# Earlier sums of x, block products for every gate pair, and low weight parts added by DMA in a two-layer hybrid decoder

## The chip, the cores and the metric

The kernel runs on one core of one Trainium2 chip. The metric is device time in microseconds (us) of one execution, the median of several runs; smaller is better. Besides the time there is a profile of one execution, with a trace of every instruction.

## The reference

Two layers work on x of 512 tokens by 1024 channels, in float32. Each layer makes one wide projection of x and feeds three mixers with it:

```python
z = einsum('bsd,de->bse', x, w_in[l])          # 1024 -> 6816 columns
(q_lat, kv_lat, k_pe, g_mla, lru_u, g_lru, r_q, r_k, r_v, g_ret, merge_logits) = split(z)
y_mla = mla(q_lat, kv_lat, k_pe, ...) * silu(g_mla)       # latent attention, 8 heads
y_lru = rglru(lru_u, ...) * silu(g_lru)                   # convolution and linear recurrence
y_ret = retention(r_q, r_k, r_v, ...) * silu(g_ret)       # 8 heads, chunks of 128 tokens
gates = sigmoid(merge_logits + b_merge[l])                # 3 x 1024 columns
mixed = sum over n of gates[n] * (y_n @ w_branch[l, n])   # each 512 -> 1024
x = layer_norm(ALPHA * x + mixed @ w_out[l])
```

## The kernel before, in words

**Three products for one.** A float32 operand is held as a high part (rounded to fp32r by a copy) and a low part (the operand less its high part). `mm3` makes high x high, high x low and low x high, so each product of tiles is three matmuls. `split` makes the two parts: a copy on ACT (L113) and a subtraction on DVE (L114). Weights come from HBM in chunks of 128 x 1024 (`load_w`): a DMA on SP's queue into a raw tile `wr` (three buffers), then `split` into `wh` and `wl` (four buffers each).

**A plain projection** of 128 output columns (`in_tile`) loads one chunk and runs 8 x 3 matmuls of 512 columns into one PSUM bank, `psmm`.

**A projection by seven products** (`in_pair`, fed by `Blocks`) makes two such tiles together in Strassen's manner. x, stored transposed as `xth`/`xtl`, is cut into four blocks: channel half k by token half t. Seven products of 12 matmuls of 256 columns each (84) replace 8 x 3 x 2 = 48 matmuls of 512. They go in the order a11, a12, s1, s2, s3, s4, a22, with two branch products b1 and b0 between them. Products a11, a12 and a22 use blocks of x as they are; s1 to s4 use four sums of such blocks, the tiles `tx`, in the order 0 to 3. `x_sums` makes these once in a layer, in four steps: each some additions on DVE (L330, L333) over 128 x 1024 elements, then `split`. The weights of s1 to s4 are sums too: two SP DMAs and one POOL DMA that adds to what is there (L383) make them in `ws`, DVE adds once more (L410), and each half chunk is split. Three PSUM tiles, `psx`, `psy1` and `psz`, are open during a pair.

**Stages of a layer.** Latent projections (`psg`); the four convolution tiles T_U; transposes of the latents (`psl`, read by DVE into `qll`/`ll`, L553); the gates T_GM and T_GL; the recurrence on ACT and DVE; queries and keys (`psq`, `psk`); attention, with the retention's values `psv` among it; retention; the gates and branches; the output projection with layer norm. In the retention's loop (`for q in range(6)`) `ret_in` makes keys and queries of two heads (tiles T_RK + t, T_RQ + t) and their rotation on DVE, `ret_keys` the scores (`psrs`, masked into `sd`), `ret_states` the running states on DVE (L757, L759), `ret_out` the output `por`.

After this loop the first four of the eight lru output tiles are made with plain projections (`in_tile` and `branch_mm`), and one step of `x_sums` stands after each; then twelve pairs by seven products follow.

**Memory.** PSUM has three pools: `ps_mm` (three banks, for `psmm`, `psx`, `psy1`, `psz`, `por`), `ps_s` (three, for `psq`, `psk`, `psb`, scores) and `ps_t` (two, for transposes). The choice between the first two is made in `PS` by the name. SBUF tiles come from rings by size: `wide` (five), `half` (four), `slot` (thirteen). A tile can be taken when an older one of its ring has had its last reader. `x_sums` takes two `wide` and four `half` before; in the retention the halves hold `rts[0..3]`, and the wides `ym`, `vr`, `tabs`, `yr`.

**Order.** A scheduler lays down each engine's instruction list when the kernel is built. It goes by the order of the code, takes what its cost model holds to be ready, and under `high_priority(offset=n)` treats instructions as if they stood n places earlier. On the chip each engine, and each DMA queue's issuer, runs its list in order and waits where an input or a buffer isn't ready.

Of the kernel before, what the change touches and what calls it, by code (L numbers as in the profile page):

```python
# [12 lines left out]
F32R = mybir.dt.float32r  # L13
# [5 lines left out]
P = 128  # L19
# [54 lines left out]
def trunk(ctx, tc, x_in, xt_in, pos, vecs, wg, wt, wrv, wuq, wuk, wuv, wlru, wbr, wout, lng, lnb, dec, rett, out):  # L74
# [37 lines left out]
    def split(hi, lo, src):  # L112
        nc.scalar.copy(hi, src)  # L113
        nc.vector.tensor_tensor(out=lo, in0=src, in1=raw(hi), op=ALU.subtract)  # L114

    def load_w(src, n, dst=None, ahead=True, dma=None, r=None):
        with tc.high_priority(offset=OFF if ahead else 0):
            if r is None:
                r = wraw.tile([P, 1024], F32, tag="wr", name="wr")
                (dma or nc.sync).dma_start(out=r[:, :n], in_=src)  # L120
            if dst is None:
                dst = (whl.tile([P, 1024], F32R, tag="wh", name="wh"), whl.tile([P, 1024], F32R, tag="wl", name="wl"))
            hi, lo = dst
            split(hi[:, :n], lo[:, :n], r[:, :n])
        return hi, lo

    def mm3(ps, lhs, rhs, start, stop, more=False):
# [170 lines left out]
    def layer(l):  # L298
        def in_tile(t):

            hi, lo = load_w(wt[l, t], 1024)
            ps = ps_mm.tile([P, S], F32, tag="mm", name="psmm")
            for k in range(KD):
                c = slice(k * P, (k + 1) * P)
                mm3(ps, (hi[:, c], lo[:, c]), xt[k], k == 0, k == KD - 1)
            return ps
# [8 lines left out]
            return [(xth[:, HK * k + j, HS * t:HS * t + HS], xtl[:, HK * k + j, HS * t:HS * t + HS]) for j in range(HK)]  # L315

        def sums(i):
            return [(tx[i][:, j, :HS], tx[i][:, j, HS:]) for j in range(HK)]

        def x_sums(tiles, scratch):  # L320

            tx[:] = tiles
            (r1, r2), (d, r4) = [(raw(t[:, :, :HS]), raw(t[:, :, HS:])) for t in scratch]

            def b(k, t):
                o = (slice(None), slice(HK * k, HK * k + HK), slice(HS * t, HS * t + HS))
                return raw(xth[o]), raw(xtl[o])

            def sub(out, a, c, op=ALU.subtract):
                nc.vector.tensor_tensor(out=out, in0=a, in1=c, op=op)  # L330

            def neg_less(out, a, c):
                nc.vector.scalar_tensor_tensor(out=out, in0=a, scalar=-1.0, in1=c[0], op0=ALU.mult, op1=ALU.subtract)  # L333
                sub(out, out, c[1])

            def less(out, a, c):
                sub(d, a[1], c[1])
                sub(out, a[0], c[0])
                sub(out, out, d, ALU.add)

            def done(i, r):
                split(tx[i][:, :, :HS], tx[i][:, :, HS:], r)

            def one():
                less(r1, b(0, 0), b(0, 1))
                done(0, r1)

            def two():
                neg_less(r2, r1, b(1, 1))
                done(1, r2)  # L350

            def three():
                less(r1, b(1, 1), b(0, 1))
                done(2, r1)

            def four():
                neg_less(r4, r2, b(1, 0))
                done(3, r4)

            return [one, two, three, four]  # L360

        class Blocks:


            def __init__(self, jobs, two):
                self.pairs = jobs
                self.two = two
                order = ("a11", "a12", "s1", "s2", "b1", "s3", "b0", "a22", "s4")
                self.jobs = [(n, m) for n, (_, wb) in enumerate(jobs) for m in order if wb is not None or m[0] != "b"]
                self.used = self.made = self.loaded = 0  # L370
                self.raws, self.ready, self.free = [], [], []

            def load(self):
                n = self.loaded
                if n == len(self.pairs):
                    return
                self.loaded += 1
                t, wb = self.pairs[n]
                d = {}
                s = self.two[:, n % 2 * 2:n % 2 * 2 + 2, :]  # L380
                nc.sync.dma_start(out=s[:, 0, :], in_=wt[l, t + 1][:, 512:])
                nc.sync.dma_start(out=s[:, 1, :], in_=wt[l, t][:, :512])
                nc.gpsimd.dma_start(out=s, in_=wt[l, t + 1][:, :512].unsqueeze(1).to_broadcast([P, 2, 512]), accum_op=ALU.add)  # L383
                d["s1"] = d["s2"] = d["s4"] = s[:, 0, :]
                d["s3"] = s[:, 1, :]
# [218 lines left out]
        for c in range(3):  # L604
            hi, lo = load_w(wuq[l, c], 768)
            for j in range(2):
                t = 2 * c + j
                ps = PS("psq")
                for k in range(3):
                    w = slice((j * 3 + k) * P, (j * 3 + k + 1) * P)  # L610
                    mm3(ps, (hi[:, w], lo[:, w]), qlat[k], k == 0, k == 2)
# [161 lines left out]
        for q in range(6):  # L773
            if q < 4:
                ret_in(q)
            if 0 <= q - 1 < 4:
                ret_keys(q - 1)
                ret_states(q - 1)
            if 0 <= q - 2 < 4:
                ret_out(q - 2)  # L780


        mixed = [slot("mixed") for _ in range(KD)]
# [23 lines left out]
            nc.gpsimd.tensor_tensor(out=rv, in0=vv, in1=mhalf, op=ALU.pow)  # L807
            nc.vector.tensor_tensor(out=y3, in0=y3, in1=rv.unsqueeze(2).to_broadcast([P, H, 64]), op=ALU.mult)


        scratch = [half("sx", F32R) for _ in range(2)]
        steps = x_sums([wide("tx", F32R) for _ in range(2)] + [half("tx", F32R) for _ in range(2)], scratch)
        for d2 in range(2):
            w = load_w(wbr[l, 1, d2], 1024)
            for j in range(2):
                d = 2 * d2 + j
                psg = in_tile(T_ME + KD + d)
                gt = slot("gt")
                nc.scalar.activation(gt, psg, AF.Sigmoid, bias=v(l, V_BM + KD + d))
                nc.vector.tensor_tensor(out=mixed[d], in0=branch_mm(w, j, yl), in1=gt, op=ALU.mult)  # L820
            steps[2 * d2]()
            steps[2 * d2 + 1]()

        def me(b, d2):
            return T_ME + b * KD + 2 * d2, wbr[l, b, d2]

        def gr(c2):
            return T_GR + 2 * c2, None

        bs = Blocks([me(1, 2), me(1, 3), me(0, 0), me(0, 1), gr(0), me(0, 2), gr(1), me(0, 3)] + [me(2, d2) for d2 in range(4)], wide("ws"))  # L830
        with tc.high_priority(offset=OFF):
            bs.load()
            bs.upto(AHEAD)
# [51 lines left out]

        yhi, ylo = half("ymh", F32R), half("yml", F32R)
        ymp = [(yhi[:, c, :], ylo[:, c, :]) for c in range(4)]
        for i in range(2):
            gate_pair(1, 2 + i, yl)
            norm_rows(i)  # L890
            for c in (2 * i, 2 * i + 1):
                split(ymp[c][0], ymp[c][1], ym[:, c, :])
# [168 lines left out]
```

## Time and profile before

| What | Value |
|---|---|
| median of 3 runs | 1042.44 us (1042.44 to 1042.65) |
| the profiled execution's own time | 1044.03 us |
| its span, first to last instruction | 1042.2 us |
| PE (TensorE matmul) busy | 1028.0 us, 99%, 6135 matmuls |
| DVE (VectorE) busy | 826.6 us, 79% |
| ACT (ScalarE) busy | 507.2 us, 49% |
| POOL (GpSimd) busy | 89.3 us, 9% |
| mean granted TensorE clock | 0.998 of full |

Matmuls are pipelined and the profile models their ends, so one matmul's duration overlaps the next one's; what a matmul costs in a full stream is the distance between starts. A row of the timeline has the start, the length, the engine, the line and what was done; a bracket at its end names how long the engine idled and what released it.

### The profile page before, as it was taken

The page shows a single profiled execution, that of the slowest core. Times are in us where ns is not written, and L with a number is a line of the kernel's source. Part 1 is how long each engine was busy: PE and PEld are TensorE (multiplying, and loading weights), DVE is VectorE, ACT ScalarE, POOL GpSimd, SP SyncE. Part 2 cuts the span into 40 slices and gives each one's busy share as a digit, 9 for nine tenths or more (in the row PEclk, how much of TensorE's full clock was granted, in tenths as well). Part 3 has the DMA queues.
Part 4 walks back from the last instruction along what each step waited for, and adds up shares of the span by engine and source line. Part 5 has one row for each costly group of instructions (what it writes and reads, how often), then busy time and mean ns, then how long its engine had stood idle before and what let it go on. Part 6 is the DMA issues. An engine that isn't in the chain of part 4 may idle for free.

```text
span 1042.2 us, 16322 instructions
## 1 busy us (share of the span) xinstructions
PE 1028.0 (99%) x6135; PEld 901.2 (86%) x6135; DVE 826.6 (79%) x1586; ACT 507.2 (49%) x963; POOL 89.3 (9%) x133
## 2 busy tenths in 40 slices
PE   9999999999999999999999999999999999999997
PEld 8877788888889999998898787888888999999986
DVE  6998989878967787687656889997789667877765
ACT  4549576511535555463223695674115445555510
POOL 1100012000102100001001000120000121000010
PEclk9999999999999999999999999999999999999999
DMA  8232431122455556525233224211214655665321
GB/s 260 81 101 86 132 112 41 43 85 76 118 149 160 160 162 195 143 91 212 75 120 102 76 78 158 79 42 63 80 62 121 206 139 140 166 201 146 120 100 61
DMA packets 46639, 123.55 MB, mean 119 GB/s; under 512 B 5088, under 2 KB 8032, under 8 KB 46560
## 3 DMA queue, kind: packets, MB, share of 16 engines
q1 hardware_dynamic: 38592, 105.39, 30.4%
q0 software_dynamic: 7680, 16.78, 8.3%
q8 instruction: 48, 0.79, 0.3%
q10 hardware_dynamic: 288, 0.34, 0.2%
q14 instruction: 31, 0.25, 0.1%
HBM read 116.20 MB, written 4.19 MB: 116 GB/s over the span
## 4 chain that ended last, share of the span: by engine, by line
PE 79%; DVE 11%; ACT 5%; issue 2%; DMA 2%; POOL 0%; SPq 0%; DVEq 0%; ACTq 0%; POOLq 0%
PE psmm L129 6%; PE psmm L130 5%; PE psmm L131 5%; PE psx L129 5%; PE psx L131 4%; PE psx L130 4%; PE psb L129 4%; PE psb L130 4%; PE psb L131 4%; PE pso L130 3%; PE pso L129 3%; PE pso L131 3%; PE psz L130 2%; PE psz L131 2%; PE psz L129 2%
## 5 line engine op out<-in xcount | busy, mean ns | idle before, releaser
L113 ACT CAST wh<-wr 128x512 fp32r<-128x512 f32 (+4 forms) x202 | 157.4, 789 | 217.4 <-PE psmm L130 122.0
L114 DVE TENSOR_TENSOR wl<-wr,wh 128x512 fp32r<-128x512 f32 (+4 forms) x202 | 179.7, 898 | 38.6 <-ACT wh L113 37.8
L129 PE MATMUL psmm<-xth,wh 128*128 128x512 f32 x384 | 151.3, 394 | 0.1
L130 PE MATMUL psmm<-xtl,wh 128*128 128x512 f32 x384 | 150.3, 391 | 0.0
L131 PE MATMUL psmm<-xth,wl 128*128 128x512 f32 x384 | 150.1, 391 | 0.0
L114 DVE TENSOR_TENSOR wl<-ws,wh 128x512 fp32r<-128x512 f32 x96 | 66.1, 689 | 46.2 <-ACT wh L113 45.4
L113 ACT CAST wh<-ws 128x512 fp32r<-128x512 f32 x96 | 59.5, 620 | 72.9 <-PE psx L130 37.8
L129 PEld LDWEIGHTS psmm<-xth,wh 128*128 128x128 f32 x384 | 72.2, 188 | 14.8 <-issue 0.4
L131 PEld LDWEIGHTS psmm<-xth,wl 128*128 128x128 f32 x384 | 72.1, 188 | 14.8
L130 PEld LDWEIGHTS psmm<-xtl,wh 128*128 128x128 f32 x384 | 72.2, 188 | 14.2
L129 PE MATMUL psx<-tx,wh 128*128 128x256 f32 x288 | 82.3, 286 | 0.3
L131 PE MATMUL psx<-tx,wl 128*128 128x256 f32 x288 | 81.5, 283 | 0.0
L130 PE MATMUL psx<-tx,wh 128*128 128x256 f32 x288 | 81.5, 283 | 0.0
L383 POOL DMA_DIRECT2D ws<-in_wt x24 | 29.1, 1220 | 399.6 <-DMA ws<-in_wt 225.9
L129 PEld LDWEIGHTS psx<-tx,wh 128*128 128x128 f32 x288 | 54.9, 191 | 4.9 <-ACT cg L446 1.1
L130 PEld LDWEIGHTS psx<-tx,wh 128*128 128x128 f32 x288 | 55.0, 191 | 1.6
L131 PEld LDWEIGHTS psx<-tx,wl 128*128 128x128 f32 x288 | 55.0, 191 | 0.0
L663 ACT ACTIVATE pr<-pss,nm 128x128 f32<-128x128 f32 (+1 forms) x64 | 34.0, 531 | 19.3 <-DVE nm L658 18.6
L656 PE MATMUL pss<-kt,qt 96*128 96x128 f32 (+3 forms) x128 | 42.1, 435 | 0.0
L129 PE MATMUL psg<-wh,xth 128*128 128x336 f32 x128 | 41.3, 323 | 0.0
L130 PE MATMUL psg<-wl,xth 128*128 128x336 f32 x128 | 40.6, 317 | 0.0
L131 PE MATMUL psg<-wh,xtl 128*128 128x336 f32 x128 | 40.5, 318 | 0.0
(308 smaller groups left out, 2822.8 us busy)
## 6 DMA issues: line engine op xcount, KB each, us to landing
wr<-in_wt SPq DMA_DIRECT2D x72, 512.0 KB, 3.4
wr<-in_wbr SPq DMA_DIRECT2D x24, 512.0 KB, 4.3
ws<-in_wt SPq DMA_DIRECT2D x48, 256.0 KB, 3.1
ws<-in_wt POOLq DMA_DIRECT2D x24, 512.0 KB, 6.6
wr<-in_wt SPq DMA_DIRECT2D x24, 256.0 KB, 3.7
wr<-in_wrv SPq DMA_DIRECT2D x8, 512.0 KB, 3.4
wor<-in_wout SPq DMA_DIRECT2D x8, 512.0 KB, 6.2
wr<-in_wout SPq DMA_DIRECT2D x8, 512.0 KB, 3.5
```

The costliest lines, as they stand in the source:

```text
L113: nc.scalar.copy(hi, src)
L114: nc.vector.tensor_tensor(out=lo, in0=src, in1=raw(hi), op=ALU.subtract)
L129: nc.tensor.matmul(ps, lh, rh, start=start, stop=False, skip_group_check=more)
L130: nc.tensor.matmul(ps, lh, rl, start=False, stop=False, skip_group_check=more)
L131: nc.tensor.matmul(ps, ll, rh, start=False, stop=stop, skip_group_check=more)
L383: nc.gpsimd.dma_start(out=s, in_=wt[l, t + 1][:, :512].unsqueeze(1).to_broadcast([P, 2, 512]), accum_op=ALU.add)
L656: nc.tensor.matmul(ps[:, :n], qt[h][:96, i * P:n], kt[h][:96, :n], start=True, stop=True)
L663: nc.scalar.activation(pr[:, :n], ps[:, :n], AF.Exp, bias=nm, scale=-1.0, accum_out=rs)
```

## The change

1. Step `one` to step `four` of `x_sums` are called inside the retention's loop, two at q = 4 and two at q = 5, after what the loop does there. `less` no longer needs a scratch tile. The sums take two `wide` and one `half`, the scratch one `half`, and the fourth sum is written over the block of x (first channel half, second token half) that no later product reads.
2. The first four lru output tiles are made by two `gate_pair` calls, so that all fourteen pairs of a layer go by seven products. For the first pair the weight sums lie in two `slot` tiles with two adding DMAs; `ws` is taken at the second pair.
3. For eleven chunks of a layer (T_U + 1 to T_U + 3, and all of T_RQ and T_RK) the low part is made by `split_acc`: ACT writes the negated high part into the low tile, and a POOL DMA reads the weight from HBM again and adds it.
4. Every second query tile (`psq2`) is in the `ps_mm` pool.

```diff
+    def split_acc(hi, lo, r, src):
+        nc.scalar.copy(hi, r)
+        nc.scalar.mul(lo, raw(hi), -1.0)
+        nc.gpsimd.dma_start(out=lo, in_=src.bitcast(F32R), accum_op=ALU.add)
...
-            split(hi[:, :n], lo[:, :n], r[:, :n])
+            if acc:
+                split_acc(hi[:, :n], lo[:, :n], r[:, :n], src)
+            else:
+                split(hi[:, :n], lo[:, :n], r[:, :n])
...
-            hi, lo = load_w(wt[l, t], 1024)
+            hi, lo = load_w(wt[l, t], 1024, acc=T_U < t < T_GL or T_RQ <= t < T_GM)
...
+        def x_sums(t1, t2, t3, scratch):
+            tx[:3] = [(t[:, :, :HS], t[:, :, HS:]) for t in (t1, t2, t3)]
+            tx[3] = (xth[:, :HK, HS:], xtl[:, :HK, HS:])
+            r1, r2 = scratch[:, :, :HS], scratch[:, :, HS:]
...
             def less(out, a, c):
-                sub(d, a[1], c[1])
                 sub(out, a[0], c[0])
-                sub(out, out, d, ALU.add)
+                sub(out, out, a[1], ALU.add)
+                sub(out, out, c[1])
...
             def four():
-                neg_less(r4, r2, b(1, 0))
-                done(3, r4)
+                neg_less(r2, r2, b(1, 0))
+                split(tx[3][0], tx[3][1], r2)
...
+                if n == 0:
+                    s0, s1 = slot("ws0"), slot("ws0")
+                elif n == 1:
+                    self.two = wide("ws")
+                if n:
+                    s = self.two[:, n % 2 * 2:n % 2 * 2 + 2, :]
+                    s0, s1 = s[:, 0, :], s[:, 1, :]
+                nc.sync.dma_start(out=s0, in_=wt[l, t + 1][:, 512:])
+                nc.sync.dma_start(out=s1, in_=wt[l, t][:, :512])
+                if n:
+                    nc.gpsimd.dma_start(out=s, in_=wt[l, t + 1][:, :512].unsqueeze(1).to_broadcast([P, 2, 512]), accum_op=ALU.add)
+                else:
+                    for sn in (s0, s1):
+                        nc.gpsimd.dma_start(out=sn, in_=wt[l, t + 1][:, :512], accum_op=ALU.add)
...
-                ps = PS("psq")
+                ps = PS("psq2" if t % 2 else "psq")
...
+            if q >= 4:
+                if q == 4:
+                    steps = x_sums(wide("tx", F32R), wide("tx", F32R), half("tx", F32R), half("sx"))
+                steps[2 * q - 8]()
+                steps[2 * q - 7]()
...
-        scratch = [half("sx", F32R) for _ in range(2)]
-        steps = x_sums([wide("tx", F32R) for _ in range(2)] + [half("tx", F32R) for _ in range(2)], scratch)
-        for d2 in range(2):
-            w = load_w(wbr[l, 1, d2], 1024)
-            for j in range(2):
-                d = 2 * d2 + j
-                psg = in_tile(T_ME + KD + d)
-                gt = slot("gt")
-                nc.scalar.activation(gt, psg, AF.Sigmoid, bias=v(l, V_BM + KD + d))
-                nc.vector.tensor_tensor(out=mixed[d], in0=branch_mm(w, j, yl), in1=gt, op=ALU.mult)
-            steps[2 * d2]()
-            steps[2 * d2 + 1]()
...
-        bs = Blocks([me(1, 2), me(1, 3), me(0, 0), me(0, 1), gr(0), me(0, 2), gr(1), me(0, 3)] + [me(2, d2) for d2 in range(4)], wide("ws"))
+        bs = Blocks([me(1, d2) for d2 in range(4)] + [me(0, 0), me(0, 1), gr(0), me(0, 2), gr(1), me(0, 3)] + [me(2, d2) for d2 in range(4)])
...
+        for i in range(2):
+            gate_pair(1, i, yl)
         for i in range(2):
             gate_pair(1, 2 + i, yl)
```

## Rows read from the trace of the kernel before

**Rows 1.** The page, part 1: engine, busy us (share of the span), instructions.

```profile
PE 1028.0 (99%) x6135; PEld 901.2 (86%) x6135; DVE 826.6 (79%) x1586; ACT 507.2 (49%) x963; POOL 89.3 (9%) x133
```

**Rows 2.** Waits of PE: waiter, what it waited for, us, times, longest.

```profile
PE psl L548 <- DVE qll L553: 1.6, 1, 1.6
PE psq L129 <- ACT qt L614: 1.6, 2, 0.8
PE warm L138 <- DVE idle L135: 1.5, 1, 1.5
PE psr L572 <- DVE xhl L569: 0.9, 4, 0.2
PE po L694 <- DVE ptl L114: 0.3, 2, 0.2
PE po L694 <- ACT pth L113: 0.3, 2, 0.2
```

**Rows 3.** Timeline of PE: first and last matmul of one plain tile (24).

```profile
272.17 0.39 PE L129 MATMUL psmm<-xth,wh 128*128 128x512 f32 x1
277.38 0.39 PE L131 MATMUL psmm<-xth,wl 128*128 128x512 f32 x1
```

**Rows 4.** Timeline of PE: first and last of two products of a pair (24 matmuls).

```profile
313.64 0.28 PE L129 MATMUL psy<-xth,wh 128*128 128x256 f32 x1
316.40 0.28 PE L131 MATMUL psz<-tx,wl 128*128 128x256 f32 x1
```

**Rows 5.** Timeline of PE: the waits at the query tiles, layer 0 and layer 1.

```profile
119.11 0.50 PE L129 MATMUL psq<-qlh,wh 128*128 128x512 f32 x1 [0.81 <-ACT qt L614]
...
634.44 0.50 PE L129 MATMUL psq<-qlh,wh 128*128 128x512 f32 x1 [0.80 <-ACT qt L614]
```

**Rows 6.** Timeline of DVE: low parts of T_U + 1 to T_U + 3, later the latent.

```profile
32.57 1.22 DVE L114 TENSOR_TENSOR wl<-wr,wh 128x1024 fp32r<-128x1024 f32 x1
...
37.87 1.23 DVE L114 TENSOR_TENSOR wl<-wr,wh 128x1024 fp32r<-128x1024 f32 x1
...
41.78 1.21 DVE L114 TENSOR_TENSOR wl<-wr,wh 128x1024 fp32r<-128x1024 f32 x1
...
62.92 0.75 DVE L553 SCALAR_TENSOR_TENSOR qll<-psl,vec,qlh 128x512 fp32r<-128x512 f32 x1
```

**Rows 7.** Windows, DVE alone: stretch, length, busy us (instructions), clock, DMA share, GB/s.

```profile
40.00:65.00 25.00, 23.18 (x59) 1.00 0.38 125
...
200.00:252.00 52.00, 37.70 (x71) 1.00 0.26 86
251.10:266.50 15.40, 15.06 (x29) 1.00 0.14 47
```

**Rows 8.** Timeline of ACT and PE: high part and first matmul, T_U + 2; retention's third chunk.

```profile
34.52 1.05 ACT L113 CAST wh<-wr 128x1024 fp32r<-128x1024 f32 x1
...
47.43 0.39 PE L129 MATMUL psmm<-xth,wh 128*128 128x512 f32 x1
...
195.23 1.05 ACT L113 CAST wh<-wr 128x1024 fp32r<-128x1024 f32 x1
...
210.00 0.39 PE L129 MATMUL psmm<-xth,wh 128*128 128x512 f32 x1
```

**Rows 9.** Tile ws: adding DMAs on POOL, min/median/max ns; landing of all its DMAs.

```profile
L383 POOL DMA_DIRECT2D ws<-in_wt x24: 1182/1196/1442, 277.3 to 952.7; - x24
...
DMA to landing us min/median/max: 2.5/4.2/10.6
```

**Rows 10.** The page, part 6: issues, KB each, median us to landing.

```profile
ws<-in_wt POOLq DMA_DIRECT2D x24, 512.0 KB, 6.6
```

**Rows 11.** Timeline of DVE at the retention's end: sums of x, the last state.

```profile
249.40 1.22 DVE L330 TENSOR_TENSOR sx<-xtl 128x1024 f32<-128x1024 f32 x1
...
266.18 0.29 DVE L759 SCALAR_TENSOR_TENSOR state<-state,retd,pskv 64x64 f32<-64x64 f32 x1
...
274.64 1.22 DVE L330 TENSOR_TENSOR sx<-sx 128x1024 f32<-128x1024 f32 x1
275.78 1.22 DVE L333 SCALAR_TENSOR_TENSOR sx<-sx,xth 128x1024 f32<-128x1024 f32 x1
```

**Rows 12.** Timeline of PE at the retention's end: keys, first plain gate tile, its end.

```profile
250.89 0.49 PE L735 MATMUL pskt<-ident,rt 128*128 128x128 f32 x3
...
261.79 0.48 PE L129 MATMUL psmm<-xth,wh 128*128 128x512 f32 x1
...
269.33 0.48 PE L131 MATMUL psmm<-xth,wl 128*128 128x512 f32 x1
```

More of the change, by code (lines that the diff above doesn't have):

```diff
@@ L114, in split, with load_w @@
         nc.vector.tensor_tensor(out=lo, in0=src, in1=raw(hi), op=ALU.subtract)
-    def load_w(src, n, dst=None, ahead=True, dma=None, r=None):
+    def split_acc(hi, lo, r, src):
+        nc.scalar.copy(hi, r)
+        nc.scalar.mul(lo, raw(hi), -1.0)
+        nc.gpsimd.dma_start(out=lo, in_=src.bitcast(F32R), accum_op=ALU.add)
+    def load_w(src, n, dst=None, ahead=True, dma=None, r=None, acc=False):
         with tc.high_priority(offset=OFF if ahead else 0):
@@ L317, in sums @@
         def sums(i):
[L318 to L323, printed above, removed]
+            return [(tx[i][0][:, j, :], tx[i][1][:, j, :]) for j in range(HK)]
+        def x_sums(t1, t2, t3, scratch):
+            tx[:3] = [(t[:, :, :HS], t[:, :, HS:]) for t in (t1, t2, t3)]
+            tx[3] = (xth[:, :HK, HS:], xtl[:, :HK, HS:])
+            r1, r2 = scratch[:, :, :HS], scratch[:, :, HS:]
             def b(k, t):
@@ L336, in less, with __init__ @@
             def less(out, a, c):
-                sub(d, a[1], c[1])
                 sub(out, a[0], c[0])
-                sub(out, out, d, ALU.add)
-            def done(i, r):
-                split(tx[i][:, :, :HS], tx[i][:, :, HS:], r)
+                sub(out, out, a[1], ALU.add)
+                sub(out, out, c[1])
             def one():
                 less(r1, b(0, 0), b(0, 1))
-                done(0, r1)
+                split(tx[0][0], tx[0][1], r1)
             def two():
                 neg_less(r2, r1, b(1, 1))
-                done(1, r2)
+                split(tx[1][0], tx[1][1], r2)
             def three():
                 less(r1, b(1, 1), b(0, 1))
-                done(2, r1)
+                split(tx[2][0], tx[2][1], r1)
             def four():
-                neg_less(r4, r2, b(1, 0))
-                done(3, r4)
+                neg_less(r2, r2, b(1, 0))
+                split(tx[3][0], tx[3][1], r2)
             return [one, two, three, four]
         class Blocks:
-            def __init__(self, jobs, two):
+            def __init__(self, jobs):
                 self.pairs = jobs
-                self.two = two
+                self.two = None
                 order = ("a11", "a12", "s1", "s2", "b1", "s3", "b0", "a22", "s4")
@@ L379, in load @@
                 d = {}
[L380 to L385, printed above, removed]
+                if n == 0:
[12 more added lines that the diff above has]
+                        nc.gpsimd.dma_start(out=sn, in_=wt[l, t + 1][:, :512], accum_op=ALU.add)
+                d["s1"] = d["s2"] = d["s4"] = s0
+                d["s3"] = s1
                 r = wraw.tile([P, 1024], F32, tag="wr", name="wr")
```

## The prediction

> **What bounds the kernel now.** I read the page's part 1 first: PE is busy 99% of the span, the next engine, DVE, 79% [rows 1]. Then the list of PE's waits, because a busy share that is modelled can hide idle time. It holds almost nothing: 1.6 us once for a DVE read of a transposed latent, 1.6 us in two waits for a query bank, and under 2 us besides after the warm-up [rows 2]. So the kernel is bound by the stream of matmuls, and only two things can shorten it: less streaming, or those two waits. Anything taken off DVE or ACT elsewhere is worth nothing by itself. Last I read the timelines, for what a matmul costs in the stream. A plain tile's 24 matmuls of 512 columns start from 272.17 to 277.38, so one costs 5.21/23 = 0.2265 us [rows 3]; 24 matmuls of 256 columns start from 313.64 to 316.40, one in 2.76/23 = 0.1200 us [rows 4]. The smaller ones cost more than half: 13 ns of each 256-column step does not shrink with the columns (2 x 0.1200 - 0.2265).
>
> **The change part by part.** *All pairs by seven products.* Each of the two pairs a layer that change loses 48 matmuls of 512 columns, 48 x 0.2265 = 10.87 us, and gets 84 of 256, 84 x 0.1200 = 10.08 us [rows 3, 4]: 0.79 us saved. The branch matmuls stay as they are. Two pairs in two layers: 4 x 0.79 = 3.2 us. This is on the path, since PE is the path. The gain is only 7% of these tiles though an eighth of the arithmetic goes.
>
> On what the small step costs a rule stands against the rows. The Trainium skill ("TensorE: Matmul & The Clock Gate", section "Back-to-back issue gap") gives a warm gap of N/2.4 ns + 2.5 ns for N columns. By it the steps would be 215.8 and 109.2 ns, a pair would save 48 x 0.2158 - 84 x 0.1092 = 1.19 us (an estimate from that page), and all four 4.7 us. The rows say 226.5 and 120.0 ns, about 11 ns more on each, so I go by them.
>
> *Two pools for queries.* The two waits of 0.81 and 0.80 us stand before the fourth query tile: three banks of ps_s are full and ACT has yet to copy the first one out [rows 5]. With every second tile in ps_mm there are six banks for six tiles. What is late next would be a ps_mm bank, which a T_GL gate still holds. Bounds: nothing (the wait changes its name) to 1.6 us. I take 1.6, because the stage before hands these banks on one tile after another. It adds nothing elsewhere.
>
> *Low parts by DMA, T_U.* In layer 0, DVE is busy 23.18 us of the 25 before 65 us [rows 7], and PE stands 1.6 us for the qll of 62.92 [rows 2, 6]. Three subtractions of 1.2 us (32.57, 37.87, 41.78) leave DVE ahead of it [rows 6]: 3 x 1.14 us, taking the distance of 275.78 and 274.64 [rows 11] for one, is 3.4 us, more than twice the wait. Waits for other engines in between can swallow part; bounds 0 to 1.6 us, and I take 1.6. Layer 1 shows no such wait, so there it is worth 0.
>
> What it adds: one ACT pass of about 1.05 us a chunk (the same shape as the cast [rows 8]) and an adding POOL DMA: issue 1.2 us [rows 9], landing 6.6 us [rows 10]. From the cast's start to a usable low part that is 1.05 + 1.05 + 1.2 + 6.6 = 9.9 us instead of some 2.3. The nearest start that must be met: T_U + 2 has its cast at 34.52 and its first matmul at 47.43, 12.9 us later; in the retention the shortest such distance I find is 195.23 to 210.00, 14.8 us, as a chunk has three others in front of it [rows 8]. So 3.0 us are left over and I cost it at nothing. The cover is the queue of weight chunks; with the longest landing of the tile's DMAs, 10.6 us [rows 9], the chain is 13.9 us and a T_U tile is 1.0 us late. On POOL's queue these DMAs wait for ACT, and behind them stand only the small powers for the norms and the adding DMAs of the first pair.
>
> *Low parts by DMA, retention.* Eight subtractions leave DVE's 37.70 busy of 52 us [rows 7]: 9.1 us more of idle time, worth nothing on PE's path by itself, but room for the next part.
>
> *The sums inside the retention.* Before, they ran beside 37 us of plain gate tiles (T_ME) and nobody waited. Now the first pair's s1 needs them. Their cost on DVE: ten additions and four low parts of 1024 elements, 14 x 1.14 = 16.0 us [rows 11], plus four ACT casts. When does PE ask? From 250.89 PE does retention work until 261.79; of the 7.5 us to 269.33 another 24 x 0.2265 = 5.4 us are the plain tile, so retention alone ends near 261.8 + 2.1 - 0.3 (a branch matmul in between) = 263.6 [rows 12]. Then a11 and a12 (2 x 1.44 us), s1 at 266.5, s2 at 267.9, b1 (12 x 0.2265 = 2.7), s3 at 272.1, b0, s4 at 276.2, a22. When does DVE deliver? From 251.1 to 266.5 it is busy 15.06 us [rows 7], of which two L330, one L333, one low part of tx and one of a weight chunk, 5 x 1.2 = 6.1 us, are not retention: 9.0 us are. Put in a row, 251.1 + 9.0 + 16.0 = 276.1, just in time for s4. The first sum needs only x, a half tile (from rts[0], whose reader is done near 240) and the fifth wide one, so it can run in idle time before 251, 4.6 us, as one addition did at 249.40 [rows 11]; that gives 271.5. The second one's tile comes free with the masks (tabs), after 260. Splits of weights (0.6 us each) and the order laid down at build time push the other way. Bounds: no wait, or 6.3 us a layer (the second rival). I take 0.5 us a layer, 1.0 in all, nearest to the row that ends in time.
>
> *Weights of the first two pairs.* a11 to s3 of the first pair can be split when the slots of the retention's last chunks come free, from 229 us on, by DVE time that the low parts left. The first pair's adding DMAs come earlier by their own slots. The second pair's `ws` needs a wide tile from vr, after the last por; two loads and an adding DMA of 6.6 us [rows 10] put it near 278 if por ends at 265, against a need at 279.1 + 2.9 = 282. I cost it at nothing; it shares the 1.0 us above.
>
> **Sum.** 3.2 + 1.6 + 1.6 - 1.0 = 5.4 us off the profiled execution's span of 1042.2 us, 1036.8; around it lie 1.8 us (1044.03). The profiled execution is 1.6 us above the median of the runs shown, 1042.44; from that the forecast is **1037.0 us**. Its own range is 1036.0 (no loss at the sums) to 1039.6 (half of the two waits, and 2 us lost at the sums).
>
> **The rivals.** *A: the two waits only change their names.* For it: DVE's chain before 63 us has waits for POOL and ACT in it, and six query banks still need ACT's copies. Against: 3.4 us taken from a wait of 1.6. Time: 1042.4 - 3.2 = 1039.2, with no loss at the sums.
>
> *B: the sums come after the retention instead of inside it, and PE waits; slower.* Place: s4, and s3, of the first pair of each layer. For it: before, three of the four sums ran behind the last state at 266.18 [rows 11], and the ring of wide tiles was one reason, which stays for the second. Price: 266.5 + 16.0 = 282.5 against a need at 276.2, 6.3 us a layer, 12.6 in all; 1042.4 - 6.4 + 12.6 = 1048.6. It decides from the point where the fourth low part comes after 279.4 in layer 0: then 3.2 us a layer eat all gains. Against: the sums now stand ahead of the pairs' work in the code, and DVE has 9.1 us less to do before.
>
> *C: low parts land too late.* With landings of 10.6 us, three T_U tiles are 1.0 us late each; with more, up to 15 us, chunks at the retention's start too. Then the gain at T_U is gone and some 2 us more: 1042.4 - 3.2 - 1.6 + 1.0 + 2 = 1040.6. For it: eleven such DMAs a layer join the twelve, and each must pass POOL's queue in order. Against: DMA is at a share of 0.26 to 0.38 in these stretches [rows 7].
> The Trainium skill ("DMA: Bandwidth & Descriptors", section "SWDGE vs HWDGE vs iDMA") speaks against these DMAs too: descriptors of POOL's DMAs are written into SBUF, from which DVE locks GpSimd out in its two-port modes, while SP's DMAs never take that way. The issues before, 1182 to 1442 ns beside a DVE that is mostly busy [rows 9], show at most 0.26 us of it.
>
> *D: in the new pairs the 13 ns that do not shrink are hidden*, and a small step costs half a large one, 0.1133 us. A pair then takes 84 x 0.1133 = 9.51 us, 1.36 less than before, and four give 5.4: 1042.4 - 5.4 - 3.2 + 1.0 = 1034.8. Against it: rows 4 are from a pair of the same form, with nothing waiting in it. The gap rule above points the same way; by its 4.7 us the time would be 1035.5.
>
> **How the numbers follow.** Forecast 0.52, A 0.15, B 0.12, C 0.13, D 0.08. A run can tell about 0.2% (2.1 us) from no change: below 1040.4 is faster, above 1044.5 slower. Faster: 0.52 + 0.14 of A + 0.05 of C + 0.08 = 0.79. Same: 0.01 of A, 0.08 of C and 0.01 of B = 0.10. Slower: 0.11 of B, from the break-even on. The range goes from 1034.0 (D with no loss at the sums gives 1033.8) to 1042.5 (C, with the sums 1 us a layer later): it leaves out B and a bit on either side.
>
> **What would show it.** Right: the matmuls of the new pairs start 0.120 us apart; no wait of PE at the fourth query tile or at psl near 62 us; DVE's L114 with 22 fewer chunks; first matmuls of T_U + 1 to + 3 and of the retention's chunks without a bracket. The sums: L330 and L333 start before 251 us and the fourth low part lies near 272 to 277 in layer 0 (some 3 us earlier if the two waits before are gone). Wrong: PE's list of waits names tx, sx or wl at psx or psz in the first two pairs (B), or the POOL DMA of a low part at psmm (C).

## The result and the profile after

The changed kernel takes 1059.32 us (four runs, 1058.18 to 1062.2) where the kernel before took 1042.55 beside it (1042.44 to 1042.92): ratio 1.0164, interval 1.0144 to 1.0185. It is slower by 16.8 us; forecast were 5.4 us off. The profiled execution took 1059.59 us, its span is 1057.8.

The page, part 1, of the kernel after, answers to [rows 1]:

```profile
PE 1029.3 (97%) x6279; PEld 907.2 (86%) x6279; DVE 821.3 (78%) x1608; ACT 539.5 (51%) x1025; POOL 109.0 (10%) x161
```

PE has 144 more matmuls: four pairs, 84 for 48 each. Its busy time went up by 1.3 us where some 3 should have gone, and its share went down by two points. The waits of PE after answer to [rows 2] (waiter, what it waited for, us, times, longest):

```profile
PE psx L138 <- ACT gt L468: 10.1, 2, 6.4
PE psx L138 <- ACT tx L113: 2.3, 2, 1.2
PE psb L140 <- DVE wl L114: 2.1, 2, 1.0
...
PE psk L138 <- ACT kt L645: 1.4, 2, 0.7
```

The wait for `qll` and those of `psq` are gone. In their place stands a new one of 1.4 us at the fourth key tile, `psk`, and 14.5 us of waits that all lie in the first two pairs of each layer.

To find where the time went I take one distance in every kernel: from the last scores of the retention (`psrs`) to the first `psy` of the third lru pair, which is a pair by seven products in both kernels. Timeline of PE, after, both layers:

```profile
255.41 1.71 PE L762 MATMUL psrs<-rt 64*128 64x128 f32 x16
...
306.55 0.28 PE L138 MATMUL psy<-xth,wh 128*128 128x256 f32 x1
...
781.10 1.71 PE L762 MATMUL psrs<-rt 64*128 64x128 f32 x16
...
829.22 0.28 PE L138 MATMUL psy<-xth,wh 128*128 128x256 f32 x1
```

The same four rows from a second profiled execution of the kernel before (1041.95 us, span 1040.2):

```profile
254.42 1.71 PE L744 MATMUL psrs<-rt 64*128 64x128 f32 x16
...
295.96 0.28 PE L129 MATMUL psy<-xth,wh 128*128 128x256 f32 x1
...
770.07 1.71 PE L744 MATMUL psrs<-rt 64*128 64x128 f32 x16
...
811.60 0.28 PE L129 MATMUL psy<-xth,wh 128*128 128x256 f32 x1
```

Before, the distance is 41.54 and 41.53 us; after, 51.14 and 48.12: 9.60 + 6.59 = 16.2 us of the 17.6 between the two spans. Everything of size is in this stretch, so the rest of the reading stays there. Layer 0, after, in the timelines: first DVE and SP, then POOL, ACT and PE; the last row is layer 1.

```profile
247.24 1.22 DVE L341 TENSOR_TENSOR sx<-xth 128x1024 f32<-128x1024 f32 x1
...
267.75 0.29 DVE L777 SCALAR_TENSOR_TENSOR state<-state,retd,pskv 64x64 f32<-64x64 f32 x1
...
284.73 1.23 DVE L114 TENSOR_TENSOR xtl<-sx,xth 128x1024 fp32r<-128x1024 f32 x1 [6.24 <-ACT xth L113]
...
269.09 0.33 SPq L395 DMA_DIRECT2D ws<-in_wt  x1
...
274.61 1.21 POOL L398 DMA_DIRECT2D ws<-in_wt  x1 [31.99 <-DMA ws<-in_wt]
...
283.13 0.62 ACT L113 CAST wh<-ws 128x512 fp32r<-128x512 f32 x1 [6.61 <-DMA ws<-in_wt]
283.65 1.04 ACT L113 CAST xth<-sx 128x1024 fp32r<-128x1024 f32 x1
284.60 0.36 ACT L468 COPY gt<-psx 128x256 f32<-128x256 f32 x1
...
268.51 0.56 PE L788 MATMUL por<-vr,sd 128*128 128x64 f32 x4
...
278.34 0.28 PE L138 MATMUL psx<-xth,wh 128*128 128x256 f32 x1
285.02 0.58 PE L138 MATMUL psx<-xth,wh 128*128 128x256 f32 x1 [6.40 <-ACT gt L468]
...
808.00 0.58 PE L138 MATMUL psx<-xth,wh 128*128 128x256 f32 x1 [3.67 <-ACT gt L468]
```

Read it backwards. PE waits for a copy of a PSUM bank on ACT. That copy has its input long since, and so has the cast ahead of it, the fourth sum of x; but both stand in ACT's list behind the cast of a `ws`, which waits 6.61 us for the adding DMA of the second pair. The DMA was issued at 274.61, after its two loads, which SP issued from 269.09 on: the `wide` tile came free with the last `por` (268.51), and that one had its state only at 267.75. The list of waits names the last link (`gt`), not the cause (`ws`).

A second cost shows in the windows of the same stretch (stretch, length, busy us of PE, PEld, DVE, ACT, POOL, granted clock, DMA share, GB/s):

```profile
274.00:280.00 6.00, 4.13 (x23) 3.40 (x23) 4.46 (x6) 2.52 (x5) 2.40 (x2) 1.00 0.83 241
280.00:286.00 6.00, 0.98 (x3) 0.96 (x4) 1.27 (x2) 2.85 (x5) 0.00 (x0) 0.66 0.76 138
286.00:292.00 6.00, 6.00 (x40) 5.81 (x40) 5.17 (x10) 3.34 (x7) 0.00 (x0) 0.77 0.00 0
```

The granted clock falls while PE stands idle and is not back when it starts again. In shorter windows it is 0.97 from 280 to 282, 0.50 from 282 to 288.6 and 1.00 from 288.8 on, so 0.66 and 0.77 are means of the chip's two levels, 1.2 and 2.4 GHz. In PE's timeline small steps start 0.21 us apart until 288.7 and 0.12 apart later:

```profile
287.20 0.41 PE L139 MATMUL psx<-xtl,wh 128*128 128x256 f32 x1
287.41 0.41 PE L140 MATMUL psx<-xth,wl 128*128 128x256 f32 x1
...
289.41 0.28 PE L139 MATMUL psx<-xtl,wh 128*128 128x256 f32 x1
289.53 0.28 PE L140 MATMUL psx<-xth,wl 128*128 128x256 f32 x1
```

### The profile page after: what moved, and what is told of

It reads as the page before. It is cut to its first block, busy times and chain, and to the rows that moved or that the text cites. A ratio compares the mean times of both kernels' runs of the same rounds, so it can differ in the third digit from the quotient of the medians.

```text
span 1057.8 us, 16761 instructions
## 1 busy us (share of the span) xinstructions
PE 1029.3 (97%) x6279; PEld 907.2 (86%) x6279; DVE 821.3 (78%) x1608; ACT 539.5 (51%) x1025; POOL 109.0 (10%) x161
## 4 chain that ended last, share of the span: by engine, by line
PE 76%; DVE 10%; ACT 8%; issue 3%; DMA 3%; SPq 0%; DVEq 0%; ACTq 0%; POOLq 0%
PE psx L138 5%; PE psx L139 5%; PE psx L140 5%; PE psmm L138 5%; PE psmm L140 5%; PE psmm L139 5%; PE psb L138 4%; PE psb L139 4%; PE psb L140 4%; PE pso L139 3%; PE pso L140 3%; PE pso L138 3%; PE psz L138 3%; PE psz L140 2%; PE psz L139 2%
## 5 line engine op out<-in xcount | busy, mean ns | idle before, releaser
L113 ACT CAST wh<-wr 128x512 fp32r<-128x512 f32 (+5 forms) x188 | 133.5, 723 | 124.4 <-PE psmm L139 42.2
L114 DVE TENSOR_TENSOR wl<-wr,wh 128x512 fp32r<-128x512 f32 (+5 forms) x188 | 151.8, 818 | 30.3 <-ACT wh L113 29.6
L138 PE MATMUL psmm<-xth,wh 128*128 128x512 f32 x320 | 125.9, 393 | 0.0
L138 PE MATMUL psx<-xth,wh 128*128 128x256 f32 x224 | 65.3, 292 | 10.2 <-ACT gt L468 10.1
L138 PEld LDWEIGHTS psmm<-xth,wh 128*128 128x128 f32 x320 | 60.1, 188 | 12.2
L138 PE MATMUL psx<-tx,wh 128*128 128x256 f32 x224 | 64.2, 286 | 2.5 <-ACT tx L113 2.3
L139 PE MATMUL psx<-xtl,wh 128*128 128x256 f32 x224 | 64.6, 288 | 0.0
L140 PE MATMUL psx<-xth,wl 128*128 128x256 f32 x224 | 63.9, 287 | 0.0
L139 PE MATMUL psx<-tx,wh 128*128 128x256 f32 x224 | 63.3, 283 | 0.0
L138 PEld LDWEIGHTS psx<-xth,wh 128*128 128x128 f32 x224 | 43.7, 195 | 12.9 <-ACT gt L468 11.1
L139 PEld LDWEIGHTS psx<-xtl,wh 128*128 128x128 f32 x224 | 44.1, 197 | 1.0
L140 PEld LDWEIGHTS psx<-xth,wl 128*128 128x128 f32 x224 | 43.6, 195 | 0.2
```

Source lines behind the costliest of these rows:

```text
L138: nc.tensor.matmul(ps, lh, rh, start=start, stop=False, skip_group_check=more)
L139: nc.tensor.matmul(ps, lh, rl, start=False, stop=False, skip_group_check=more)
L140: nc.tensor.matmul(ps, ll, rh, start=False, stop=stop, skip_group_check=more)
```

## The experiments

My theory T after the result: the whole loss is the second pair's weight sums, which land near 283 us. Rivals: DVE, which is full here since the sums of x moved in; the eleven adding DMAs of the low parts; one of the other parts of the change.

**slots2: the second pair's weight sums in slot tiles too.**

```diff
-                if n == 0:
+                if n < 2:
                     s0, s1 = slot("ws0"), slot("ws0")
-                elif n == 1:
+                elif n == 2:
                     self.two = wide("ws")
...
```

> The changed kernel, with the weight sums of the second pair of each layer in two slot tiles as those of the first (ws is taken at the third pair). Theory T (the second pair's weight sums come late, because their wide tile waits for the last retention output; ACT's list has their cast in front of the fourth sum's, and PE stands): the waits of 6.4 us (layer 0) and 3.7 us (layer 1) at psx go, with some 2 us of slow clock after them; 1059 falls to about 1047 (1045 to 1050). Rival R1 (the sums of x themselves come too late, DVE is the limit): the fourth sum's additions end at the same time, the wait shrinks by 2 us at most; 1055 to 1059. Rival R2 (the adding DMAs and ACT passes for the low parts of the 11 chunks cost it): no change, 1057 to 1061.

Measured: 1047.1 us, ratio 1.0041 (1.0026 to 1.0056). POOL's timeline has the second pair's adding DMAs 18 to 25 us earlier, and PE's first product with these sums runs at 284.65 without a wait:

```profile
249.87 0.87 POOL L401 DMA_DIRECT2D ws<-in_wt  x1 [7.80 <-DMA ws<-in_wt]
256.62 0.86 POOL L401 DMA_DIRECT2D ws<-in_wt  x1 [5.88 <-DVE state L775]
...
284.65 0.28 PE L138 MATMUL psz<-tx,wh 128*128 128x256 f32 x1
```

Its waits of PE, and the distance in layer 0:

```profile
PE psx L138 <- ACT tx L113: 2.3, 2, 1.2
PE psb L140 <- DVE wl L114: 2.1, 2, 1.0
...
254.86 1.71 PE L762 MATMUL psrs<-rt 64*128 64x128 f32 x16
...
298.31 0.28 PE L138 MATMUL psy<-xth,wh 128*128 128x256 f32 x1
```

The waits of 6.4 and 3.7 us are gone, and 12.2 of the 16.8 us with them: theory T holds for these, not for the whole loss. What stays is 1.17 us for `tx` and 1.03 us for `wl` in each layer. The distance defined above is now 43.45 us in both layers, 1.9 more than before.

**sums_first40: the steps of the sums treated as standing 40 places earlier.**

```diff
-                steps[2 * q - 8]()
-                steps[2 * q - 7]()
+                with tc.high_priority(offset=40):
+                    steps[2 * q - 8]()
+                    steps[2 * q - 7]()
```

> The changed kernel, with the four steps of the sums placed 40 instructions earlier in the order, so that ACT's list has the fourth sum's cast ahead of the second pair's weights. Theory T: the fourth sum no longer stands behind the late weights, but the weights are still late for the second pair; a wait of 1 to 4 us a layer stays; 1046 to 1053. R1: the same or better, 1043 to 1048, with no wait left at the second pair. R2: 1057 to 1061.

Measured: 1064.99 us, ratio 1.0223 (1.0203 to 1.0242). Missed, in the other direction. The sums took DVE from the states and scores of the retention's end: the last state came at 277.39, after 267.75 in the changed kernel. The last `por`, and with it the `wide` tile, came later with it, and SP's loads of `ws` left at 279.06 in place of 269.09:

```profile
279.06 0.33 SPq L395 DMA_DIRECT2D ws<-in_wt  x1
```

So DVE's load matters twice: for the sums, and for the moment at which the tile of the weight sums comes free.

**no_acc: low parts on DVE again, by `load_w(wt[l, t], 1024)`.**

> The changed kernel, with the low parts of all chunks by DVE again (no added DMAs for them). Theory T: the waits at the second pair stay and the wait at the latent's transposes of layer 0 comes back (1.6 us); 1059 to 1063. R1: DVE has 9 us more to do ahead of the sums, so the wait grows; 1062 to 1070. R2: most of the loss goes; 1043 to 1050.

Measured: 1061.67 us, ratio 1.0184 (1.0169 to 1.0199), within the interval of the change's own ratio. The wait stays and is longer (13.7 us in two), which R1 had foretold for a DVE with more to do. The trace gives another reason: in layer 0 the wait is 6.34 us, as in the changed kernel, and in layer 1, where it is 7.35, the time from the adding DMA's issue to the cast was 10.2 us (798.10 to 808.25) instead of 7.4 (798.73 to 806.12). The adding DMAs of the low parts are not the cause. The wait at `psl`, which T expected back, did not come.

**no_pairs: the first four lru tiles plain as before, the sums still in the retention.**

```diff
...
+        for d2 in range(2):
+            w = load_w(wbr[l, 1, d2], 1024)
+            for j in range(2):
+                d = 2 * d2 + j
+                psg = in_tile(T_ME + KD + d)
...
-        for i in range(2):
-            gate_pair(1, i, yl)
```

> The changed kernel, with the first four lru tiles by plain projections again, placed behind the retention; sums inside the retention, low parts by DMA and two query pools stay (the fourth sum has a half tile of its own, as the plain projections read the block it would overwrite). Theory T: nobody needs the sums or ws early, no wait there; what the other parts bring stays: 1039 to 1042. R1: the same. R2: 1048 to 1060.

Measured: 1045.38 us, ratio 1.0025 (1.0015 to 1.0034). Missed: without the pairs the rest gains nothing and costs 2.8 us. In its trace, the stretch to the third pair's `psy` is as before; PE then loses 0.57 and 0.44 us at that pair, for a `wl` and a `wh` of a `ws` that ACT had waited 1.48 us for. From this pair's `psy` to the next one's the two layers are 1.69 and 1.00 us longer than before, nearly all of the loss. The late `ws` is the main theme on a small scale.

**cast_behind: after, with one cast moved in ACT's list.** The cast of the second pair's first `ws` is put behind the cast of the fourth sum and the copy at L468, its two victims above.

```diff
-                split(hl[0], hl[1], d[m])
+                with tc.issue_after(self.gt) if n == 1 and m == "s1" else tc.high_priority(offset=0):
+                    split(hl[0], hl[1], d[m])
...
```

> The changed kernel with one instruction of ACT's list placed otherwise in each layer: the cast of the second pair's first weight sum stands behind the fourth sum's cast and the copy of psx, two places later. All data come as late as before. Theory T1 (the loss is the place in ACT's list: PE had enough other work, the late weights only block what stands behind them): the waits of 6.4 and 3.7 us go, and the slow clock behind the first; 1059 falls to about 1047, as with slot tiles (1045 to 1050). Rival T2 (the weights themselves are too late for the second pair): PE waits for them a little later; about 4 us a layer stay, 1052 to 1058.

Measured: 1062.57 us, ratio 1.0185 (1.0164 to 1.0206); its runs lie from 1057.18 to 1063.58. Both expected ranges were missed. ACT and PE of this kernel:

```profile
283.01 0.62 ACT L113 CAST wh<-ws 128x512 fp32r<-128x512 f32 x1 [4.98 <-DMA ws<-in_wt]
283.54 0.61 ACT L113 CAST wh<-wr 128x512 fp32r<-128x512 f32 x1
...
284.20 0.80 PE L138 MATMUL psb<-yl,wh 128*128 128x512 f32 x1 [5.50 <-ACT wh L113]
```

I first took this as proof that the sums land too late for their own use. The rows say something else: PE waits for the `wh` of a `wr`, and that cast is simply the next victim in ACT's list. So one more kernel was made.

**cast_third: the same landing, the two first `ws` casts of the second pair behind that cast too.**

```diff
...
+                if n == 1 and m in ("s1", "s2"):
+                    self.later.append((hl, m))
+                else:
+                    put(hl, m)
+                if n == 1 and m == "b1":
+                    with tc.issue_after(self.gt):
+                        for job in self.later:
+                            put(*job)
...
```

> The kernel after with the weight sums where they were (wide tile, loads at 269, landing near 283 us); in ScalarE's list alone the two casts of the second pair's first two weight sums now stand behind the cast of that pair's b1 as well as behind the cast of the fourth sum and the copy of the first pair's bank (cast_behind left the b1 cast waiting behind the first of them, and TensorE waited 5.8 us for that one). Theory O (order: nothing needs the sums themselves before about 285 us, only what stands behind their cast waits): the waits of 6.4 and 3.7 us go and none of their size comes, the time is that of slots2, 1046 to 1049. Theory L (the landing at 283 is itself too late for the products): a wait of 3 us or more a layer comes back at psz or psb for wh or wl, 1056 to 1062.

Measured: 1054.41 us, ratio 1.0108 (1.0095 to 1.0122); its runs lie far apart, 1050.19 to 1055.59, and the profiled execution is the lowest of them. The expected 1046 to 1049 was missed by all of them. ACT, and PE's first product of the second pair with a `ws`:

```profile
277.94 0.63 ACT L113 CAST wh<-wr 128x512 fp32r<-128x512 f32 x1
282.50 1.14 ACT L113 CAST wh<-ws 128x512 fp32r<-128x512 f32 x2 [3.94 <-DMA ws<-in_wt]
283.66 1.28 ACT L865 ACT_TABLE_LOAD   x1
...
285.49 0.39 PE L138 MATMUL psy<-xth,wh 128*128 128x256 f32 x1 [1.73 <-ACT gt L865]
...
287.03 0.28 PE L138 MATMUL psz<-tx,wh 128*128 128x256 f32 x1
```

The sums land at 282.5, much as in the other two, yet PE's wait is 1.73 us (0.74 in layer 1) where it was 6.40 (3.67), and again for something behind these casts, the reading of a gate's bank, ahead of which a table load of 1.28 us stands too. The products with the sums themselves (287.03) wait for nothing. The distance is 45.47 and 44.42 us, so 9.4 of the 16.2 us lost in the two stretches are back (slots2: 12.4). In the profiled execution, then, the mechanism of theory O holds: most of the loss is the place of a waiting cast in an in-order list. That execution is the fastest of five; by the median only 4.9 of the 16.8 us are back, so that order alone is most of the loss isn't shown for the others. Where these lose up to 5.4 us more isn't shown either. The spread would fit a landing that varies, and from issue to cast it did vary from 7.4 to 10.2 us between the traces of the changed kernel and no_acc. In cast_behind and cast_third a few entries behind the moved casts, in the lists of ACT, DVE and SP, changed places too; what that is worth isn't shown.

**psq2_alone, acc_alone, before_again: the two small parts by themselves, and the kernel before a second time.** psq2_alone is the kernel before with the one line `ps = PS("psq2" if t % 2 else "psq")`; acc_alone is it with `split_acc` for the eleven chunks.

> The kernel before with only the second pool for every other query tile. As predicted: the two waits of 0.8 us go, 1.6 us less (1040.9). Rival (from the changed kernel's trace): a wait of 0.7 us at the keys takes the place of each, and the attention that follows gives the rest back: no change, 1042.0 to 1043.5.

> The kernel before with only the low parts of the 11 chunks a layer by ACT and an adding DMA. As predicted: the wait at the latent's transposes goes, 1.6 us less (1040.9). Rival V (that wait belongs to the one profiled execution, which took 1044.03 us, 1.6 above the median): nothing to win, 1042.0 to 1043.5. Rival C (low parts too late): 1044 to 1048, with PE waiting for the adding DMA at psmm.

> The kernel before, profiled once more. Rival V expects no wait of PE at psl and a profiled execution near 1042.4 us; if the wait is there in every execution, 1.6 us at psl again.

Measured: psq2_alone 1042.37 us, ratio 1.0000 (0.9991 to 1.0009); acc_alone 1042.68 us, ratio 1.0005 (0.9996 to 1.0014); before_again 1041.95 us. Waits of PE, first in psq2_alone, then in before_again:

```profile
PE psk L129 <- ACT kt L627: 1.5, 2, 0.8
```

```profile
PE psq L129 <- ACT qt L614: 1.6, 2, 0.8
```

Both parts are worth nothing. The bank of a query tile isn't waited for any more, but a bank of `psk` is, as long. And the wait for `qll` is missing in the second execution of the unchanged kernel, whose time is 2.1 us below the first profiled one (in psq2_alone it is 0.3 us): the 1.6 us belonged to that one execution, not to the kernel.

**sums_early and pairs_only: what is left over in slots2.** sums_early is slots2 with the first sum called at q = 3, the second at q = 4, the others at q = 5; pairs_only is slots2 with one pool for queries and the low parts on DVE.

> The kernel of slots2 with its first sum of x one retention step earlier (q = 3, the second at q = 4 in a half tile, the third and fourth at q = 5). In slots2 VectorE is busy 34.2 of the 40 us to 290 us without a gap from 246 us on, while it idles 4.6 us before 244. Theory S (what is left over in slots2 is a VectorE that is full in this stretch, so low parts of weights and the third sum come late): the waits psb for wl (1.0 us a layer) and psx for tx (1.2 us a layer) go or halve, 1047.1 becomes 1043 to 1045. Rival R (the order of ScalarE's list or the change between steps of 256 and 512 columns, not VectorE): the first sum moves, the waits keep their size, 1046.5 to 1047.5.

> The kernel of slots2 without the second pool for queries and without the low parts by DMA: what stays is the pairs with the sums of x in the retention. Theory T (those two parts are worth nothing, alone as well as here): within 1 us of slots2, 1046 to 1048. Rival P (the low parts by DMA relieve VectorE where the sums need it): slower than slots2 by 2 us or more, with the waits for wl and tx grown. Rival Q (the two parts cost about 0.7 us a layer in the attention, as slots2 stands there against the kernel before): 1045 to 1046.

Measured: sums_early 1048.32 us, ratio 1.0058 (1.0045 to 1.0070); pairs_only 1046.5 us, ratio 1.0038 (1.0024 to 1.0051). (DVE is busy 39.28 us of the 40 to 290 in slots2; the 34.2 in the expectation is wrong.) sums_early did not test what it was made for: in its trace the first sum starts at 247.44, behind the same rotation as in slots2 (246.69), since the scheduler placed it there. The wait for `wl` is 0.57 us in place of 1.03 and that for `tx` is gone, but a bank's copy is waited for instead (0.69), `por` waits for its state (0.35), and the time is 1.2 us longer. These waits don't explain it: the distance is 43.17 and 43.19 us, 0.28 and 0.26 less than in slots2, so the added time lies outside this stretch, 0.67 us of it in layer 0 ahead of the first plain tile (36.59 for 35.92). pairs_only, with the same waits for `tx` and `wl`, says for the second time that the two small parts don't help.

**half_pairs and half_pairs_first: one pair more by seven products, not two.** The first two lru tiles stay plain, and the sums stand behind them as before; `ws` of the new pair lies in two slots. As in the kernel before, there is one pool for queries and DVE makes all low parts.

```diff
...
+        w = load_w(wbr[l, 1, 0], 1024)
+        for d in range(2):
+            psg = in_tile(T_ME + KD + d)
...
+            steps[2 * d]()
+            steps[2 * d + 1]()
...
-        for i in range(2):
-            gate_pair(1, i, yl)
+        gate_pair(1, 1, yl)
```

> Between the two kernels: the first two lru gate tiles stay plain (two steps of the sums behind each of them, after the retention as in the kernel before), only the second pair of the four tiles goes by seven products, its weight sums in two slot tiles; the wide tile for weight sums is taken from the third pair on. One pool for queries, low parts on VectorE. Theory W (the pair is worth its 0.79 us as soon as its weight sums and the sums of x have the 10.9 us of a plain pair in front of them): no wait at the first pair, one pair a layer saved, 1042.6 - 2 x 0.79 = 1041.0 us (1040.5 to 1041.8). Rival V (a pair costs more than it saves whenever it stands so early, by changes between steps of 256 and 512 columns or by a full VectorE): 1042.5 to 1045.

Measured: 1053.53 us, ratio 1.0106 (1.0089 to 1.0123). Missed by 12 us. In SP's timeline the slots' loads are the fifth and sixth of six that leave together; the four before them go to the `wide` tile of later pairs and wait for the last `por`. The cast and PE's product follow from that:

```profile
268.48 0.33 SPq L395 DMA_DIRECT2D ws<-in_wt  x1
...
270.33 0.38 SPq L395 DMA_DIRECT2D ws<-in_wt  x1
270.81 0.36 SPq L396 DMA_DIRECT2D ws<-in_wt  x1
...
284.57 0.62 ACT L113 CAST wh<-ws 128x512 fp32r<-128x512 f32 x1 [3.78 <-DMA ws<-in_wt]
...
285.25 0.38 PE L138 MATMUL psz<-tx,wh 128*128 128x256 f32 x1 [3.43 <-ACT wh L113]
```

half_pairs_first takes, loads and adds the two slots before the tiles for `mixed` are taken, and nothing else:

```diff
+            def early(self):
+                t = self.pairs[0][0]
+                self.pre = slot("ws0"), slot("ws0")
...
+        with tc.high_priority(offset=OFF):
+            bs.early()
         mixed = [slot("mixed") for _ in range(KD)]
```

> half_pairs once more, with the two slot tiles of the first pair's weight sums taken, loaded and added to before the tiles for mixed, so that on SyncE these two loads stand ahead of the loads into the wide tile (in half_pairs they stood behind four of them and left only at 270.3, after the last por; the casts of ws waited till 284.6). Theory W2 (that order alone cost half_pairs its loss): no wait of psz for wh, the loads leave before 268, 1041.0 us (1040.5 to 1041.8). Rival V (an early pair costs more than it saves even then): 1042.5 to 1046, with other waits at the first pair.

Measured: 1041.51 us beside 1042.54, ratio 0.9990 (0.9981 to 0.9999). SP and PE, both layers:

```profile
247.67 0.42 SPq L384 DMA_DIRECT2D ws<-in_wt  x1
...
254.93 1.26 PE L768 MATMUL psrs<-rt 64*128 64x128 f32 x12
...
295.69 0.28 PE L138 MATMUL psy<-xth,wh 128*128 128x256 f32 x1
...
769.83 1.37 PE L768 MATMUL psrs<-rt 64*128 64x128 f32 x13
...
810.59 0.28 PE L138 MATMUL psy<-xth,wh 128*128 128x256 f32 x1
```

The loads leave at 247.67 and the new pair waits for nothing. The distance is 40.76 us in both layers, 0.78 and 0.77 less than before; in half_pairs it was 46.39 and 47.15, with 3.43 and 3.46 us of waits and a granted clock of 0.73 from 286 to 292. Two loads, with their adds, moved ahead of four on one queue are worth 12.0 us here, and this is the only kernel of the study that is faster than the one before, by 1.0 us.

## Why the prediction was wrong, point by point

**The step that failed** is "two loads and an adding DMA of 6.6 us [rows 10] put it near 278 if por ends at 265, against a need at 279.1 + 2.9 = 282. I cost it at nothing". Both sides of it were off, and the term measured 12.2 us: that is what slots2 gains, in which the second pair's weight sums lie in slot tiles and land earlier.

- *The landing.* The last state came at 267.75 [rows 11 had it at 266.18], so SP loaded from 269.09; the loads took until 274.61, and the adding DMA 8.5 us more (274.61 to 283.13) at a DMA share near 0.8. Two adds of 512 KB and two more chunks were under way together. I had used the median of 6.6, though the trace had landings up to 10.6 [rows 9]. Five us late in all.
- *The need.* I took the moment at which PE uses the sums. What counts is the place of their cast in ACT's list: there it stood ahead of a sum of x, a bank's copy and a weight cast that PE wanted from 278.4 on. cast_third, with nearly the same landing (282.50), waits 1.73 us in place of 6.40 in its profiled execution. This was a question of ACT's list, and I had asked only about data.
- *The price.* 6.40 + 3.67 us of waits, and the lower granted clock after them. In layer 0 the loss of 9.60 us is 6.40 + 1.17 + 1.02 of waits, less 2 x 0.79 = 1.58 saved, which leaves 2.6 us that no wait holds; slots2, at a granted clock of 1.00, has 1.3 us of that sort (1.91 + 1.58 - 2.20). So the lower clock cost some 1.3 us there, an estimate by difference. Most of the other 1.3 us stands at changes of shape: where the scheduler puts small steps between the branch's large ones and the retention's, the step at a change takes longer (in slots2 a small one starts at 268.34 and a large one at 268.55, 0.21 us in place of 0.12). Added up in layer 0, the steps at such changes stand 1.50 us over 0.1200 and 0.2265 us each in slots2, 0.52 in the second profile of the kernel before and 0.53 in half_pairs_first. So 1.0 of the 1.3 us are a price of the interleaving, for which the sum had no term; 0.3 stay open.

No rival had this either. B put the loss at the right place, s4 of the first pair, and its signs came (`tx` at `psx` in the list of waits, the fourth low part at 284.73, past 279.4), but it got the wrong mechanism: the sums of x would be late on DVE, while DVE stood idle for 6.24 us there until ACT's cast. Its time, 1048.6, is near slots2 by coincidence of size only; there the waits for `tx` and `wl` are 2.2 us a layer, not 6.3.

**Seven products: right.** 0.79 us a pair was forecast from [rows 3, 4], and half_pairs_first measures 0.78 and 0.77; of these 1.55 us, 1.0 shows in its median. The gap rule of the Trainium skill ("TensorE: Matmul & The Clock Gate", "Back-to-back issue gap"), which the page gives for an isolated matmul and not for a stream, would have made it 1.19, an estimate from that page; the rows decide against it here.

**Two query pools, 1.6 us: nothing.** The bound "the wait changes its name" was the true end. The bank that is late next is `psk`'s.

**Low parts in T_U, 1.6 us: nothing.** I subtracted a wait of the one profiled execution from a median that didn't hold it. That this execution lay 1.6 us above the median, which the prediction itself notes, was the sign: the wait of 1.6 us that stood once [rows 2, 6] was the difference. Rival A thus held for both terms, 3.2 of the forecast 5.4 us.

**Low parts in the retention, and rival C: right that they cost nothing.** acc_alone stands at 1.0005, and no `psmm` waits for such a DMA.

**The sums: in time in their start, mis-sized in their price.** The first began at 247.24 (forecast: before 251), and in slots2 the fourth low part starts at 277.88 (forecast: 272 to 277), without holding up the pairs by much. But they fill DVE, 39.28 us of 40, and 2.2 us of waits a layer stand beside it, where I had put 0.5. That a full DVE makes these waits is theory S; no run confirmed it.

## What to carry to other kernels

When a step is moved earlier, ask not only when its data arrive and when they are used, but what stands behind its first instruction in every in-order list it passes: a cast that waits for a DMA on ACT, or four loads that wait for a tile on SP, stop everything after them. A tile ring decides when a transfer may start, so follow each new tile back to the last reader of the old one, and take the long landings for the stretch in which it will run. A wait that stands once in one profiled execution is worth nothing until a second execution shows it.

## What the hardware showed that I had not expected

- Within 6.4 us without a matmul the granted clock fell to 0.50, the lower level, and it stayed there until 288.6, through the restart at 285.02. Small steps took 0.21 us instead of 0.12 until 3.7 us after the restart. In half_pairs, after 3.43 us without one, the window from 286 to 292 is at 0.73. In cast_third, whose idle time was 1.73 us, the three windows of this stretch are all at 1.00.
- An adding DMA of 512 KB took 8.5 us from issue to use at a DMA share near 0.8, against a median of 6.7 over the 26 of this kernel; the longest landing of all DMAs of `ws` was 8.9 us, in slots2 9.5.
- The place of two loads and their adds among the DMA issues, in kernels with the same arithmetic, moved the time by 12.0 us (1053.53 to 1041.51); the two pairs it serves are worth 1.6.
